# A decoder trunk on one core: values behind logits, queries' transposes behind the probabilities', two fill places a block

## The chip, the cores and the metric

The kernel runs on one core of a Trainium2 chip. The time is device microseconds of one execution of the whole program. The kernel before was run three times: median 1867.74 us, between 1866.12 and 1868.64.

## The reference

Two layers over 1024 tokens of width 1024, all in float32. The first is a gated DeltaNet layer, the second cross-attention in a sliding window of 128 tokens, with 32 query heads of width 64 in groups of eight on 4 key and value heads. The change lies in the second layer. Cut to it:

```python
def swa_sink_mixer(h, w_in, q_gain, sinks, w_out, k_band, v_band, bias, mask):
    q, z = jnp.split(h @ w_in, 2, axis=-1)                       # projections
    q = rms_norm(q.reshape(B, T, B_Q_HEADS, B_HD), q_gain) * (B_HD ** -0.5)
    logits = jnp.einsum("bnqkgd,bnskd->bnkgqs", q, k_band) + bias
    logits = jnp.where(mask, logits, -jnp.inf)
    m = jnp.maximum(jnp.max(logits, axis=-1, keepdims=True), sink)
    p = jnp.exp(logits - m)
    probs = p / (jnp.sum(p, axis=-1, keepdims=True) + jnp.exp(sink - m))
    o = jnp.einsum("bnkgqs,bnskd->bnqkgd", probs, v_band)
    return (o.reshape(B, T, B_W) * jax.nn.silu(z)) @ w_out
```

The tokens come in 8 blocks of 128; the queries of block n see the keys of the blocks n-1 and n.

## The kernel before, in words

Float32 products are made from two halves of each operand, `hi` and `lo`: hi times hi, hi times lo, lo times hi, three matmuls for one.

The second layer's work is cut into 8 head groups (`Group`, four query heads each) of 8 token blocks, 64 blocks in all. A block goes through four pieces on TensorE, and each piece has its followers on other engines:

- `q_turn(i)`: two transposes of the queries (L1149, tile `tp`). ScalarE writes them out as `qT` (L1152), VectorE the rest as `qTl` (L1153).
- `logits(i)`: six pairs of matmuls (L1174, tile `lg`). A pair uses the two halves of the array's rows at the same time. VectorE applies the window (L1178) and adds the bias and takes the extreme `m` (L1182), ScalarE makes the exponentials and their sums (L1187), VectorE the reciprocal `den` (L1189), GpSimd the probabilities `lsb` (L1191).
- `turn(i)`: four transposes of the probabilities (L1197, tile `tp`), written out by ScalarE (L1201) and VectorE (L1205) as `pT`; GpSimd masks the part of the earlier block (L1202).
- `values(i)`: products of `pT` with the values (L1218, tile `pv`), pairs that use the two halves of the array's columns; a block with n = 0 has half as many. ScalarE writes them out as `ot` (L1220).

Between these pieces stand the projections: of the queries (`b_q`, through `gemm_tc`, L983 to L985, 256 columns a matmul) and of the gate z (`b_z`, through `gemm_ct`, L180, L182, L184, 512 columns a matmul), tile `mm`. TensorE's instructions stay in the order in which the code is written. The order is made by `interleave`: the generator `b_attend` is the front and yields a number in places where it can be filled, and the projections are the back and are taken until their costs have used up that number (0.65 for six matmuls of the queries, about 0.22 for one of z). The four pieces of one pass of the loop belong to different blocks: `turn(i)`, `q_turn(i + 3)`, `logits(i + 2)`, `values(i - 1)`. The order on the other engines is set by a scheduler that puts the front's instructions ahead of the back's.

PSUM holds three tiles `tp`, two pairs of `lg`, one `pv` and two `mm`.

Of the kernel before, what the change touches and what calls it, by code (L numbers as in the profile page):

```python
# [64 lines left out]
class Kernel:  # L65
# [1072 lines left out]
    def b_attend(self, groups):  # L1138
# [5 lines left out]
        def q_turn(i):  # L1144
            X, n = blocks[i]
            qv = X.q[n // 4][:, n % 4, :, :].rearrange("p (r a) d -> p r (a d)", a=2)
            ps = aps.tile([P, 4, P], F32, name="tp", bufs=3)[:, 0:2, :]
            for pr in range(2):
                nc.tensor.transpose(out=ps[:, pr, :], in_=qv[:, pr, :], identity=self.ident)  # L1149
            hi = bp.tile([P, 2, P], F32R, name="qT")  # L1150
            lo = bp.tile([P, 2, P], F32R, name="qTl")
            nc.scalar.copy(out=hi, in_=ps)  # L1152
            nc.vector.tensor_tensor(out=lo, in0=ps, in1=self.f32(hi), op=ALU.subtract)  # L1153
            qT[i] = hi, lo
# [38 lines left out]
        def turn(i):  # L1193
            L = Ls.pop(i)
            ps = aps.tile([P, 4, P], F32, name="tp", bufs=3)
            for e in range(4):
                nc.tensor.transpose(out=ps[:, e, :], in_=L[:, e, 0:P], identity=self.ident)  # L1197
            pTs[i] = {}
            if blocks[i][1]:
                pT = pTs[i][0] = bp.tile([P, 4, P], F32, name="pT0")  # L1200
                nc.scalar.copy(out=pT, in_=ps)  # L1201
                nc.gpsimd.affine_select(out=pT, in_=pT, pattern=[[0, 4], [-1, P]], compare_op=ALU.is_gt, fill=0.0,  # L1202
                                        base=0, channel_multiplier=1)
            pT = pTs[i][1] = bp.tile([P, 4, P], F32, name="pT1")
            nc.vector.tensor_tensor(out=pT, in0=ps,  # L1205
                                    in1=self.cst[:, C_TRI:C_TRI + P].unsqueeze(1).broadcast_to([P, 4, P]), op=ALU.mult)

        def values(i):
            X, n = blocks[i]
            g, c = X.hg // 2, n % 4  # L1210
            if c == 0:
                X.ot.append(bp.tile([P, 2, 512], F32, name="ot", bufs=4))
            po = aps.tile([P, 2, P], F32, name="pv", bufs=1)
            pT = pTs.pop(i)
            for kb in sorted(pT, reverse=True):
                v = self.vv[:, n - 1 + kb, g * 64:g * 64 + 64]
                for e in range(2):
                    nc.tensor.matmul(po[e * 64:e * 64 + 64, :, :], v, pT[kb][:, e::2, :],  # L1218
                                     start=(kb == 1), stop=(kb == min(pT)))
            nc.scalar.activation(out=X.ot[-1][:, :, c * P:c * P + P], in_=po, func=AF.Copy, scale=0.5)  # L1220
            if n == NB - 1:
                self.b_done(X)
# [7 lines left out]
        logits(1)  # L1230
        q_turn(2)
        yield 2.5
        fill = (1.2, 1.2, 0.6, 0.6, 1.2)
        steps = iter(())
        for i, (X, n) in enumerate(blocks):
            turn(i)
            yield fill[0]
            if i + 3 <= last:
                q_turn(i + 3)
            yield fill[1]  # L1240
            if i + 2 <= last:
                logits(i + 2)
            yield fill[2]
            if X.hg < 7:
                nxt = groups[X.hg + 1]
                if n == 0:
                    nxt.keys, steps = self.key_stack(nxt.hg // 2) if X.hg % 2 else (X.keys, iter(()))
                    self.b_bias(nxt)
                next(steps, None)
            yield fill[3]  # L1250
            if i:
                values(i - 1)
            yield fill[4]
        values(last)

    def run(self):
# [142 lines left out]
```

## Time and profile before

| what | value |
|---|---|
| median of three runs | 1867.74 us |
| profiled execution, its own time | 1867.72 us |
| its span, first to last instruction | 1866.0 us |
| granted TensorE clock over the span | 0.996 |
| TensorE matmuls, busy | 1809.7 us (97%) |
| VectorE busy | 1231.2 us (66%) |
| ScalarE busy | 730.7 us (39%) |
| GpSimd busy | 514.0 us (28%) |

The busy time is the union of the instructions' spans, from the first to the last instruction of the program. Matmuls overlap in time, so a duration printed for one is longer than the distance to the next; to see how fast TensorE moves, starts are compared with starts. The second layer's attention lies between about 1154 and 1690 us. Before it come the first layer and the keys and values, behind it the output projection.

### The profile page before, as it was taken

How to read it: one execution, taken by the hardware profiler on the slowest of the kernel's cores; microseconds unless marked ns; L12 is line 12 of the kernel's file. 1: busy time of each engine (PE TensorE's matmuls, PEld its weight loads, DVE VectorE, ACT ScalarE, POOL GpSimd, SP SyncE). 2: the span in 40 equal slices, each digit the busy share in tenths (PEclk: the TensorE clock that was granted, in tenths of full speed). 3: DMA queues.
4: the chain of work that ended last, by engine and by line, in shares of the span. 5: the costliest groups of instructions: out<-in, count | busy, mean ns of one | idle time of the engine just before them, and what ended most of it. 6: DMA issues, size and time to landing. Idle time of an engine off the chain costs nothing.

```text
span 1866.0 us, 31106 instructions
## 1 busy us (share of the span) xinstructions
PE 1809.7 (97%) x11778; PEld 1466.0 (79%) x11778; DVE 1231.2 (66%) x2895; ACT 730.7 (39%) x1813; POOL 514.0 (28%) x629
## 2 busy tenths in 40 slices
PE   6999999999999998999999999999999999999999
PEld 6667778787878776778788899887787787777887
DVE  6777776868586778765545365777776766763432
ACT  6446362634445364523112042444444444441100
POOL 1323232323222233221311231333333323221211
PEclk9999999999999999999999999999999999999999
DMA  4611111112011111122655331111111111225552
GB/s 151 134 49 35 57 46 46 47 35 69 23 58 35 58 34 47 45 91 92 236 170 171 122 92 46 30 46 46 63 41 52 57 34 59 68 69 201 182 169 102
DMA packets 134874, 149.55 MB, mean 80 GB/s; under 512 B 7242, under 2 KB 91716, under 8 KB 134724
## 3 DMA queue, kind: packets, MB, share of 16 engines
q1 hardware_dynamic: 124384, 130.40, 22.5%
q10 hardware_dynamic: 10340, 17.16, 2.9%
q8 instruction: 93, 1.52, 0.3%
q14 instruction: 57, 0.47, 0.1%
HBM read 116.05 MB, written 31.49 MB: 79 GB/s over the span
## 4 chain that ended last, share of the span: by engine, by line
PE 77%; DVE 10%; issue 3%; POOL 3%; ACT 1%; DMA 1%; POOLq 0%; DVEq 0%; ACTq 0%; SPq 0%
PE mm L180 9%; PE mm L182 9%; PE mm L184 9%; PE acc L933 6%; PE acc L932 6%; PE acc L931 6%; PE mm L983 4%; PE mm L984 4%; PE mm L985 4%; PE pv L1218 3%; PE lg L1174 3%; DVE acc L494 2%; PE tp L1197 1%; DVE wlo L157 1%; PE kqp L693 1%
## 5 line engine op out<-in xcount | busy, mean ns | idle before, releaser
L180 PE MATMUL mm<-hh,whi 128*128 128x512 f32 (+1 forms) x1040 | 428.0, 412 | 2.5 <-ACT hh L246 2.4
L182 PE MATMUL mm<-hl,whi 128*128 128x512 f32 (+1 forms) x1040 | 417.9, 402 | 1.5 <-DVE hl L247 1.5
L184 PE MATMUL mm<-hh,wlo 128*128 128x512 f32 (+1 forms) x1040 | 415.4, 399 | 0.0
L157 DVE TENSOR_TENSOR wlo<-wraw,whi 128x512 fp32r<-128x512 f32 x292 | 205.8, 728 | 225.0 <-POOL whi L150 192.4
L150 POOL TENSOR_SCALAR whi<-wraw 128x1024 fp32r<-128x1024 f32 x110 | 121.3, 1103 | 474.7 <-PE acc L933 240.7
L180 PEld LDWEIGHTS mm<-hh,whi 128*128 128x128 f32 x1040 | 197.0, 189 | 39.1 <-issue 4.6
L184 PEld LDWEIGHTS mm<-hh,wlo 128*128 128x128 f32 x1040 | 196.9, 189 | 37.3 <-issue 4.2
L182 PEld LDWEIGHTS mm<-hl,whi 128*128 128x128 f32 x1040 | 197.2, 190 | 35.6 <-issue 4.2
L983 PE MATMUL mm<-whi,hh 128*128 128x256 f32 x608 | 183.6, 302 | 0.0
L984 PE MATMUL mm<-wlo,hh 128*128 128x256 f32 x608 | 171.9, 283 | 0.0
L985 PE MATMUL mm<-whi,hl 128*128 128x256 f32 x608 | 171.8, 283 | 0.0
L494 DVE SCALAR_TENSOR_TENSOR acc<-u,cw,acc 128x512 f32<-128x512 f32 x192 | 152.9, 798 | 22.0 <-POOL acc L491 19.6
L1187 ACT ACTIVATE lsb<-lsb,m 128x129 f32<-128x129 f32 x256 | 100.4, 394 | 165.2 <-DVE m L1182 129.3
L983 PEld LDWEIGHTS mm<-whi,hh 128*128 128x128 f32 x608 | 115.8, 190 | 14.7 <-issue 10.0
L1191 POOL TENSOR_TENSOR lsb<-lsb,den 128x512 f32<-128x512 f32 x64 | 72.9, 1139 | 189.2 <-DVE den L1189 177.6
L153 POOL TENSOR_TENSOR wraw<-wraw,gcolb 128x512 f32<-128x512 f32 x72 | 79.0, 1117 | 140.4 <-DMA wraw<-in_b_w_in 96.7
L984 PEld LDWEIGHTS mm<-wlo,hh 128*128 128x128 f32 x608 | 116.1, 191 | 0.2
L985 PEld LDWEIGHTS mm<-whi,hl 128*128 128x128 f32 x608 | 115.8, 190 | 0.0
L491 POOL TENSOR_SCALAR acc<-u,cw 128x512 f32<-128x512 f32 x64 | 57.0, 891 | 183.4 <-ACT u L487 169.9
L931 PE MATMUL acc<-whi,hh 128*128 128x512 f32 x256 | 99.7, 389 | 0.0
L933 PE MATMUL acc<-whi,hl 128*128 128x512 f32 x256 | 99.6, 389 | 0.0
L932 PE MATMUL acc<-wlo,hh 128*128 128x512 f32 x256 | 99.6, 389 | 0.0
(352 smaller groups left out, 3722.0 us busy)
## 6 DMA issues: line engine op xcount, KB each, us to landing
wraw<-in_a_w_in SPq DMA_DIRECT2D x48, 512.0 KB, 4.0
wraw<-in_a_w_out SPq DMA_DIRECT2D x32, 512.0 KB, 3.6
wraw<-in_b_w_in SPq DMA_DIRECT2D x32, 512.0 KB, 4.0
wraw<-in_b_w_out SPq DMA_DIRECT2D x32, 512.0 KB, 3.9
og<-zs SPq DMA_DIRECT2D x32, 256.0 KB, 2.0
ogT<-zs SPq DMA_DIRECT2D x24, 256.0 KB, 2.1
btab<-lt SPq DMA_DIRECT2D x1, 4096.0 KB, 24.3
dm<-gd SPq DMA_DIRECT2D x8, 512.0 KB, 4.1
```

Of the source, the lines that this page charges most:

```text
L150: nc.gpsimd.tensor_scalar(out=hi, in0=raw, scalar1=1.0, scalar2=1.0, op0=ALU.mult, op1=ALU.mult)
L157: nc.vector.tensor_tensor(out=lo[:, ks], in0=raw[:, ks], in1=self.f32(hi[:, ks]), op=ALU.subtract)
L180: nc.tensor.matmul(ps, hi[:, k, :], hh[:, k, :], start=(k == 0), stop=False)
L182: nc.tensor.matmul(ps, hi[:, k, :], hl[:, k, :], start=False, stop=False)
L184: nc.tensor.matmul(ps, lo[:, k, :], hh[:, k, :], start=False, stop=(k == KT - 1))
L494: nc.vector.scalar_tensor_tensor(out=acc, in0=u[:, t:t + 512], scalar=cw[:, t, blk:blk + 1], in1=acc, op0=ALU.mult, op1=ALU.add)
L931: nc.tensor.matmul(ps[c], oh[:, k, ts], hi[:, kk, :], start=(k4 + k == 0), stop=False)
L932: nc.tensor.matmul(ps[c], oh[:, k, ts], lo[:, kk, :], start=False, stop=False)
L933: nc.tensor.matmul(ps[c], ol[:, k, ts], hi[:, kk, :], start=False, stop=(k4 + k == 6))
L983: nc.tensor.matmul(ps, hh[:, k, ts], hi[:, k % 4, :], start=(k == 0), stop=False)
L984: nc.tensor.matmul(ps, hh[:, k, ts], lo[:, k % 4, :], start=False, stop=False)
L985: nc.tensor.matmul(ps, hl[:, k, ts], hi[:, k % 4, :], start=False, stop=(k == KT - 1))
```

## The change

One pass of the loop in `b_attend` is written in another order. `q_turn(i + 3)` follows `turn(i)` without a yield between, `values(i - 1)` follows `logits(i + 2)` without one, and the yields become 2.4, 1.2 and 1.2 in place of 1.2, 1.2, 0.6, 0.6 and 1.2. The key steps and the bias load of the next head group stand behind the values, between the last two yields. Nothing is computed in another way.

```diff
-        fill = (1.2, 1.2, 0.6, 0.6, 1.2)
         steps = iter(())
         for i, (X, n) in enumerate(blocks):
             turn(i)
-            yield fill[0]
             if i + 3 <= last:
                 q_turn(i + 3)
-            yield fill[1]
+            yield 2.4
+
             if i + 2 <= last:
                 logits(i + 2)
-            yield fill[2]
+            if i:
+                values(i - 1)
+            yield 1.2
             if X.hg < 7:
                 nxt = groups[X.hg + 1]
                 if n == 0:
                     nxt.keys, steps = self.key_stack(nxt.hg // 2) if X.hg % 2 else (X.keys, iter(()))
                     self.b_bias(nxt)
                 next(steps, None)
-            yield fill[3]
-            if i:
-                values(i - 1)
-            yield fill[4]
+            yield 1.2
         values(last)
```

The order on TensorE behind the logits of one block, in the kernel before; `mm` rows are projections of z, `lg` logits, `pv` values:

```order
L1174 MATMUL lg<-kl,qT 128x256 x2
L184 MATMUL mm<-hh_85,wlo 128x512
L180 MATMUL mm<-hh_85,whi 128x512
L182 MATMUL mm<-hl_86,whi 128x512
L184 MATMUL mm<-hh_85,wlo 128x512
L180 MATMUL mm<-hh_85,whi 128x512
L182 MATMUL mm<-hl_86,whi 128x512
L1218 MATMUL pv<-pT_12028,vv 64x256 x2
L1218 MATMUL pv<-pT_12025,vv 64x256 x2
```

The same place on TensorE in the changed kernel:

```order
L1174 MATMUL lg<-kl,qT 128x256 x2
L1218 MATMUL pv<-pT_12028,vv 64x256 x2
L1218 MATMUL pv<-pT_12025,vv 64x256 x2
L184 MATMUL mm<-hh_85,wlo 128x512
L180 MATMUL mm<-hh_85,whi 128x512
L182 MATMUL mm<-hl_86,whi 128x512
```

The six projections that stood between the logits and the values stand behind the values. The transposes that follow on TensorE, before; `lsb` are the probabilities, `qr` the queries:

```order
L1197 MATMUL tp<-cst,lsb 128x128 x4
L182 MATMUL mm<-hl_86,whi 128x512
L184 MATMUL mm<-hh_85,wlo 128x512
L180 MATMUL mm<-hh_85,whi 128x512
L182 MATMUL mm<-hl_86,whi 128x512
L184 MATMUL mm<-hh_85,wlo 128x512
L180 MATMUL mm<-hh_85,whi 128x512
L1149 MATMUL tp<-cst,qr 128x128 x2
L182 MATMUL mm<-hl_86,whi 128x512
```

And in the changed kernel:

```order
L1197 MATMUL tp<-cst,lsb 128x128 x4
L1149 MATMUL tp<-cst,qr 128x128 x2
L182 MATMUL mm<-hl_86,whi 128x512
L184 MATMUL mm<-hh_85,wlo 128x512
L180 MATMUL mm<-hh_85,whi 128x512
```

The six projections between the two groups of transposes stand behind both.

## Rows read from the trace of the kernel before

**Rows 1.** Stretches: length; busy of PE, PEld, DVE, ACT, POOL; granted clock; DMA share; GB/s.

```profile
1163.20:1168.80 5.60, 5.60 (x29) 5.24 (x30) 4.93 (x18) 2.47 (x11) 4.02 (x3) 0.50 0.00 0
1170.00:1690.00 520.00, 520.00 (x3701) 415.25 (x3700) 371.23 (x1196) 241.64 (x776) 171.76 (x229) 1.00 0.18 55
```

**Rows 2.** Waits of 1150 to 1690: who waited for whom, total us, times, longest.

```profile
PEld pv L1218 <- issue: 12.9, 36, 0.4
...
PE lg L1174 <- DVE m L1182: 3.2, 2, 1.7
```

**Rows 3.** Timeline of TensorE, logits and values among query projections: start, length, instruction.

```profile
1302.69 0.28 PE L985 MATMUL mm<-whi,hl 128*128 128x256 f32 x1
1302.90 0.38 PE L1174 MATMUL lg<-kh,qT 64*128 64x256 f32 x2
1303.12 0.28 PE L1174 MATMUL lg<-kh,qTl 64*128 64x256 f32 x2
...
1303.60 0.28 PE L1174 MATMUL lg<-kl,qT 64*128 64x256 f32 x2
1303.81 0.39 PE L983 MATMUL mm<-whi,hh 128*128 128x256 f32 x1
1304.03 0.28 PE L984 MATMUL mm<-wlo,hh 128*128 128x256 f32 x1
1304.15 0.28 PE L985 MATMUL mm<-whi,hl 128*128 128x256 f32 x1
...
1305.21 0.28 PE L985 MATMUL mm<-whi,hl 128*128 128x256 f32 x1
1305.42 1.08 PE L1218 MATMUL pv<-pT,vv 128*64 128x256 f32 x8
1306.44 0.39 PE L983 MATMUL mm<-whi,hh 128*128 128x256 f32 x1
1306.66 0.28 PE L984 MATMUL mm<-wlo,hh 128*128 128x256 f32 x1
```

**Rows 4.** Timeline of TensorE, values of a block with n = 0.

```profile
1313.34 0.65 PE L1218 MATMUL pv<-pT,vv 128*64 128x256 f32 x4
1313.92 0.39 PE L983 MATMUL mm<-whi,hh 128*128 128x256 f32 x1
```

**Rows 5.** Timeline of TensorE, logits among z projections of 512 columns.

```profile
1669.34 0.28 PE L1174 MATMUL lg<-kl,qT 64*128 64x256 f32 x2
1669.55 0.50 PE L180 MATMUL mm<-hh,whi 128*128 128x512 f32 x1
1669.88 0.39 PE L182 MATMUL mm<-hl,whi 128*128 128x512 f32 x1
1670.12 0.39 PE L184 MATMUL mm<-hh,wlo 128*128 128x512 f32 x1
```

**Rows 6.** Timeline of TensorE, start of the stage, transposes directly behind logits.

```profile
1157.51 0.27 PE L1174 MATMUL lg<-kl,qT 64*128 64x128 f32 x2
1157.71 0.44 PE L1149 MATMUL tp<-cst,qr 128*128 128x128 f32 x2
1157.91 0.37 PE L983 MATMUL mm<-whi,hh 128*128 128x256 f32 x1
```

**Rows 7.** Timeline of TensorE, transposes among query projections.

```profile
1307.85 0.28 PE L985 MATMUL mm<-whi,hl 128*128 128x256 f32 x1
1307.97 0.60 PE L1197 MATMUL tp<-cst,lsb 128*128 128x128 f32 x4
1308.33 0.36 PE L983 MATMUL mm<-whi,hh 128*128 128x256 f32 x1
1308.53 0.28 PE L984 MATMUL mm<-wlo,hh 128*128 128x256 f32 x1
...
1309.82 0.38 PE L1149 MATMUL tp<-cst,qr 128*128 128x128 f32 x2
1309.96 0.36 PE L983 MATMUL mm<-whi,hh 128*128 128x256 f32 x1
```

## The prediction

> **What bounds the kernel now.** I read the stretch table first, because the page's share of busy time averages over stages and the change touches one: attention of the second layer, from about 1154 us to 1690 us. From 1170 us on TensorE is busy for 520.00 of 520.00 us at a granted clock of 1.00, while VectorE has 371 us of work, ScalarE 242 and GpSimd 172 [rows 1]. Then the waits, to see whether TensorE stands for anyone: its matmul queue waits 3.2 us in all, twice, for the maxima `m` of VectorE, and both waits lie at the start of the stage, before 1170 us; what its weight loads are charged with is "issue", which is a wait for nothing the profile shows [rows 2]. So the stage lasts as long as TensorE's own sequence, and only what happens between two neighbouring matmuls can shorten it. That is why the third view was the timeline of TensorE alone, read by the distance from one start to the next.
>
> In the projections of the queries a matmul of 256 columns follows the last after 0.12 us (1304.03 to 1304.15). At the logits this breaks [rows 3]. The last projection starts at 1302.69, the first pair of logits at 1302.90: 0.21, or 0.09 more than the beat. The second pair starts 0.22 after the first, 0.10 more. The last pair at 1303.60 is followed by a projection at 1303.81, 0.09 more; and the projection after that comes 0.22 later, 0.10 more. The shape printed in the rows says what is special: projections use the array as 128*128, logits as 64*128, value products as 128*64. Each time the shape changes, the next group starts 0.09 us late and its first interval is stretched as well. The values show it too: 0.09 before (1305.21 to 1305.42), 0.10 after the first projection behind them (1306.44 to 1306.66). A block with four value rows lasts 0.58 up to the next projection [rows 4], one with eight 1.02, so four rows (two pairs) are worth 0.44 and 0.58 - 0.44 = 0.14 is overhead: 0.09 of it the late start of what follows, 0.05 the stretched first interval, half as long as the others.
>
> So alone among projections a logits group carries 0.09 + 0.10 + 0.09 + 0.10 = 0.38 us of overhead, and a values group 0.09 + 0.14 + 0.10 = 0.33, together 0.71 us a block. In the stretch with 512-column projections (beat 0.24, 1669.88 to 1670.12) the way out of the logits is the same: the usual 0.12 becomes 0.21, and the first projection takes 0.33 in place of 0.24 [rows 5]. About half of the blocks lie in each stretch.
>
> **The change part by part.** (a) *Values directly behind logits.* The order of instructions on TensorE has this neighbourhood in the blocks 1 to 61 (block 0 has no values before it, the last two no logits): 61 times a return to the 128*128 shape between the two groups disappears. What goes is the 0.09 and 0.10 on the way out of the logits and the 0.09 + 0.05 on the way into the values, 0.33 us. What comes is one direct boundary from 64*128 to 128*64, which before never had. Its bounds: nothing at all if neither shape has to wait for the other, and 0.33 us if it costs as much as both old boundaries. The nearest row is at the start of the stage, where logits are followed directly by transposes: 1157.51 to 1157.71 is 0.20, again 0.09 late, and the two transposes take 0.20 to the next projection [rows 6] where 0.14 is usual [rows 7], so 0.06 more: 0.15 in all. Every boundary in rows 3 is a late start of 0.09, whatever the two shapes, plus a first interval that depends on the incoming group (0.10 for logits and projections, 0.05 for values). I therefore take 0.09 + 0.05 = 0.14 and a gain of 0.33 - 0.14 = 0.19 us a block: 61 x 0.19 = 11.6 us. The ends are 61 x 0.33 = 20.1 us and zero.
>
> On such boundaries the Trainium skill, "TensorEngine Tiling (Array Packing)", section Tiling Modes (Key Properties), says that changing the tiling mode drains TensorE, while changing only the tile does not. The trace agrees as to the late start of 0.09 us at every change of shape. The page names the drain alone; by it the change would save one drain a block, 61 x 0.09 = 5.5 us, and the stretched first interval behind each boundary, which rows 3 show, would not be counted.
>
> (b) *Queries' transposes directly behind the probabilities'.* This looks like the same gain and is not. Transposes have the projections' shape 128*128. Four of them start on the beat (1307.85 to 1307.97), reach the next projection after 0.36 and stretch its first interval to 0.20, 0.08 more [rows 7]: 0.44 for four. Two take 0.14 and the same 0.08: 0.22. That is 0.11 us for each transpose and nothing for the group, so six in a row cost 0.66 = 0.44 + 0.22. I put this part at zero, 61 times.
>
> (c) *Two fill places.* The fill of a block stays 1.2 + 1.2 + 0.6 + 0.6 + 1.2 = 2.4 + 1.2 + 1.2 = 4.8, so the same projections are spread over the same blocks; no matmul is added or removed, and none changes its operands.
>
> (d) *What moves on the other engines.* The pair of `q_turn` evictions (ScalarE `qT`, VectorE `qTl`) comes right behind those of `turn`, and ScalarE's copy of the values `ot` now comes ahead of the four exponentials of the same block, or in front of most of them, instead of between or behind them. The bias loads on SP and the key steps come one place later. All of it is covered by TensorE's projections: the maxima of a block are needed one block later, when its logits' PSUM tiles are reused, its probabilities between one and two blocks later, and the fill between logits and the `turn` that reads them is 7.2 before and after. If that cover went, every late microsecond would be a microsecond of the stage, since TensorE has no slack of its own. I cost it at zero.
>
> The sum: the profiled execution took 1867.72 us, 1866.0 of them the span, and the median of the runs is 1867.74, so the two can be used alike. 1867.7 - 11.6 = 1856.1 us.
>
> **The rivals.**
> *The direct boundary is free.* Rows and columns of the array are split differently in the two groups, and if the values' weights can be brought in under the last logits, all 0.33 us go: 1867.7 - 20.1 = 1847.6 us. Against it: in the rows no change of shape starts on the beat.
> *The direct boundary is dear.* It changes both the row and the column split, which no row shows, and could cost two late starts and two stretched intervals. Between one that leaves 0.09 us of gain (5.5 us, 1862.2) and one that leaves nothing (1867.7). For it speaks only that it was never seen; against it, that 0.09 appears alike at all boundaries of rows 3 and 6.
> *A new wait, and a slow clock behind it (slower).* The one place where TensorE waited is the second block of logits: it needed the PSUM tiles that VectorE had not yet read out, and stood for 3.2 us [rows 2]; behind that the granted clock was 0.50, the 1.2 GHz level, for 5.6 us [rows 1], half of which, 2.8 us, is lost. Such an event costs 6.0 us. Now the evictions come in two bursts in place of four places a block, so VectorE or ScalarE may read out the logits later than before. If the reordering brought one such event at each of the seven changes of head group, where VectorE also has key and gate work, it would cost 42 - 11.6 = 30 us: 1898 us. At two events the gain is gone, and three, 1867.7 - 11.6 + 18 = 1874.1 us, are the nearest clear loss. Against it: after 1170 us the whole 520 us have no such wait, with VectorE busy 71% of the time.
>
> **How the numbers follow.** The forecast, 61 boundaries less at 0.19 us, gets 0.70, with its own range of 1853 to 1860 (0.13 to 0.24 us a block, the rounding of four differences of 0.01 and a microsecond or two of new waits). The free boundary gets 0.10, the dear one 0.15, of which 0.07 for about 1862 and 0.08 for no gain, and the new wait 0.05. What a measurement of this kernel can tell from no change is about 0.2%, 3.7 us. Faster than 1864.0 are the forecast, the free boundary and the milder dear one: 0.87. Within 0.2% is the dear one without gain: 0.08. Slower is the wait: 0.05. The range runs from 1849 to 1863: it holds the forecast, the milder dear boundary and the part of the free one that falls short of its end, and leaves out some 0.18.
>
> **What would show it.** In the profile after, the last pair of logits and the first value product should start about 0.21 us apart, the first interval within the values stay at its present length, and the next projection follow as now. The six transposes should last about 0.58 us to the next projection, 0.36 + 2 x 0.11. The stage should end some 11 to 12 us earlier with TensorE still busy all the time at clock 1.00, and everything after it, the output projection, shift without changing its length. I am wrong if the distance from logits to values is well over 0.21 us or at the beat of 0.12, if waits of TensorE for `m`, `lsb`, `qT` or a free PSUM tile appear after 1170 us, or if the clock falls inside the stage.

## The result and the profile after

The changed kernel takes 1856.36 us (median of five runs, 1851.54 to 1859.02), the kernel before 1867.84 in the runs beside it: 11.5 us less, ratio 0.9935 with a 95% interval of 0.992 to 0.9949. The forecast was 1856.1. Runs with the same mean granted clock, 0.995, lie further apart than the medians: 1856.07 to 1857.62 us with the change, 1868.97 to 1872.03 before (those measured beside e1 to e4).

The stretch of attention and the waits of TensorE in the kernel after, read as [rows 1] and [rows 2]:

```profile
1170.00:1679.00 509.00, 509.00 (x3713) 419.80 (x3713) 369.61 (x1206) 240.97 (x783) 174.92 (x231) 1.00 0.18 56
```

```profile
PE lg L1174 <- DVE m L1182: 3.2, 2, 1.7
...
PEld pv L1218 <- issue: 1.1, 3, 0.4
```

TensorE is busy all the time, as before, at a granted clock of 1.00 once a slow stretch at the start has ended (at about 1172.2 us here), and its matmuls wait for nothing but the maxima at the start, the same 3.2 us. The weight loads of the values were charged with 12.9 us of "issue" before, and with 1.1 us now: 61 of 64 times they no longer follow projections.

The timeline of TensorE in the kernel after, one pass of the loop among query projections; it answers to [rows 3] and [rows 7]:

```profile
1302.41 0.28 PE L985 MATMUL mm<-whi,hl 128*128 128x256 f32 x1
1302.62 0.38 PE L1174 MATMUL lg<-kh,qT 64*128 64x256 f32 x2
1302.85 0.28 PE L1174 MATMUL lg<-kh,qTl 64*128 64x256 f32 x2
...
1303.32 0.28 PE L1174 MATMUL lg<-kl,qT 64*128 64x256 f32 x2
1303.53 1.08 PE L1218 MATMUL pv<-pT,vv 128*64 128x256 f32 x8
1304.55 0.39 PE L983 MATMUL mm<-whi,hh 128*128 128x256 f32 x1
1304.77 0.28 PE L984 MATMUL mm<-wlo,hh 128*128 128x256 f32 x1
1304.89 0.28 PE L985 MATMUL mm<-whi,hl 128*128 128x256 f32 x1
...
1307.38 0.28 PE L985 MATMUL mm<-whi,hl 128*128 128x256 f32 x1
1307.50 0.60 PE L1197 MATMUL tp<-cst,lsb 128*128 128x128 f32 x4
1307.93 0.38 PE L1149 MATMUL tp<-cst,qr 128*128 128x128 f32 x2
1308.07 0.37 PE L983 MATMUL mm<-whi,hh 128*128 128x256 f32 x1
1308.27 0.28 PE L984 MATMUL mm<-wlo,hh 128*128 128x256 f32 x1
```

The direct boundary that no row of before showed: 1303.32 to 1303.53, 0.21, late by the usual 0.09. From there the values last 1.02 to the next projection, as in [rows 3], so their stretched first interval has kept its 0.05. The way from logits back to projections (0.09 and 0.10) is gone. The six transposes take 0.57 to the next projection, whose first interval is then stretched to 0.20, 0.08 more than usual: 0.65 in all, where four and two apart took 0.44 + 0.22 = 0.66.

From the first transposes of the probabilities to the first matmul of the output projection the profile before has 517.92 us (1169.87 to 1687.79) and the one after 504.86 (1172.86 to 1677.72), 13.06 less. What follows is 178.17 and 178.16 us long. The two profiled executions, 1867.72 and 1857.62, differ by only 10.1 us because the attention began 2.84 us later in the second; the code before it is the same, and in the ten profiles of this study its first logits lie anywhere from 1155.9 to 1160.9 us. A part of that is the clock ahead of the attention: the three profiles with the earliest starts (before, e3, e8) have two short stretches at a granted clock of 0.50 there, the changed kernel three, and e5, the latest, five. I therefore compare this stage, called *the stage* below, beside the medians.

### The profile page after: what moved, and what is told of

Read it like the earlier page. It is cut to its first block, busy times and chain, and to the rows that moved or that the text cites. A ratio compares the mean times of both kernels' runs of the same rounds, so it can differ in the third digit from the quotient of the medians.

```text
span 1855.9 us, 31123 instructions
## 1 busy us (share of the span) xinstructions
PE 1798.2 (97%) x11778; PEld 1469.2 (79%) x11778; DVE 1228.8 (66%) x2895; ACT 729.0 (39%) x1813; POOL 518.7 (28%) x629
## 4 chain that ended last, share of the span: by engine, by line
PE 76%; DVE 10%; issue 4%; POOL 3%; ACT 1%; DMA 1%; POOLq 0%; ACTq 0%; DVEq 0%; SPq 0%
PE mm L180 9%; PE mm L182 9%; PE mm L184 9%; PE acc L932 6%; PE acc L933 6%; PE acc L931 6%; PE mm L983 4%; PE mm L985 4%; PE mm L984 4%; PE pv L1218 3%; PE lg L1174 3%; DVE acc L494 2%; PE tp L1197 2%; DVE wlo L157 1%; PE kqp L693 1%
## 5 line engine op out<-in xcount | busy, mean ns | idle before, releaser
L983 PE MATMUL mm<-whi,hh 128*128 128x256 f32 x608 | 178.4, 293 | 0.0
L983 PEld LDWEIGHTS mm<-whi,hh 128*128 128x128 f32 x608 | 116.1, 191 | 11.2 <-issue 10.8
L153 POOL TENSOR_TENSOR wraw<-wraw,gcolb 128x512 f32<-128x512 f32 x72 | 82.7, 1169 | 143.1 <-DMA wraw<-in_b_w_in 77.9
```

The costliest lines, as they stand in the source:

```text
L983: nc.tensor.matmul(ps, hh[:, k, ts], hi[:, k % 4, :], start=(k == 0), stop=False)
```

## The experiments

| kernel | median us | ratio to before (95%) | stage us |
|---|---|---|---|
| before | 1867.84 | | 517.92 |
| the change | 1856.36 | 0.9935 (0.992 to 0.9949) | 504.86 |
| e1 values behind logits alone | 1856.13 | 0.9934 (0.992 to 0.9947) | 505.38 |
| e2 transposes joined alone | 1868.68 | 0.9995 (0.9986 to 1.0004) | 517.50 |
| e3 values behind transposes | 1867.24 | 0.9991 (0.9983 to 1.0) | 517.75 |
| e4 values ahead of logits | 1855.82 | 0.9926 (0.9912 to 0.994) | 504.80 |
| e8 values in two parts | 1874.33 | 1.0031 (1.0021 to 1.0041) | 524.07 |
| e6 values of two blocks | 1849.92 | 0.9907 (0.9894 to 0.9921) | 500.50 |
| e5 later second logits | 1852.48 | 0.9917 (0.9905 to 0.993) | 503.51 |
| e7 e5 and e6 | 1849.48 | 0.99 (0.9886 to 0.9913) | 500.71 |

The runs of before beside e1 to e4 had a median of 1869.46, those beside e5 to e8 1868.57, so ratios are compared. The stage of e5 and e7 can't be set beside the others as it stands: 1.2 of fill was moved ahead of its beginning.

**e1 and e2: which half of the change gains.** All diffs from here on are against the changed kernel, some of them cut; e1 separates the transposes again, e2 the logits and the values.

```diff
             turn(i)
+            yield 1.2
             if i + 3 <= last:
                 q_turn(i + 3)
-            yield 2.4
+            yield 1.2
```

> Only half of the change: values directly behind logits, the queries' transposes in their old place with 1.2 of fill before them; three places a block. Theory (a return to the 128*128 shape between logits and values costs 0.19 us net, joined transposes cost nothing less): the whole gain, 61 x 0.19 = 11.6 us, ratio to before 0.994, as long as the full change. Rival 'breaks' (each interruption of the projections costs the same, the change took two of four away, 11.5 us / 122 = 0.094 us each): only 5.7 us, ratio 0.997.

```diff
                 logits(i + 2)
-            if i:
-                values(i - 1)
-            yield 1.2
+            yield 0.6
...
                 next(steps, None)
+            yield 0.6
+            if i:
+                values(i - 1)
             yield 1.2
```

> The other half alone: queries' transposes directly behind the probabilities', logits and values apart as before with 1.2 of fill between them. Theory: nothing, since transposes have the projections' shape: 61 x 0.01 us at most, ratio 1.000. Rival 'breaks': 5.7 us, ratio 0.997. A rival by the order on the other engines (the joined evictions help or hurt) would show waits of TensorE.

e1 has the whole gain at three places a block, e2 none at three places. Had every interruption of the projections cost the same, the two would have gained alike. TensorE's matmuls wait for nothing after 1170 us in either, so the order on the other engines is no cause.

**e3: two places a block, but no change of shape less.**

```diff
                 q_turn(i + 3)
+            if i:
+                values(i - 1)
             yield 2.4

             if i + 2 <= last:
                 logits(i + 2)
-            if i:
-                values(i - 1)
             yield 1.2
```

> Two places a block as in the change, but the values stand behind the transposes and not behind the logits, so the shape goes 128*128, 128*64, 128*128, 64*128, 128*128: as many changes of shape as before. Theory: no gain, 0.71 us of overhead a block as before, ratio 1.000 (1867 us). Rival 'breaks': the whole gain, 11.5 us, ratio 0.994.

The timeline of TensorE in e3, the way out of the logits and the values behind the transposes:

```profile
1296.25 0.28 PE L1174 MATMUL lg<-kl,qT 64*128 64x256 f32 x2
1296.46 0.38 PE L983 MATMUL mm<-whi,hh 128*128 128x256 f32 x1
1296.68 0.28 PE L984 MATMUL mm<-wlo,hh 128*128 128x256 f32 x1
...
1299.12 0.38 PE L1149 MATMUL tp<-cst,qr 128*128 128x128 f32 x2
1299.44 1.08 PE L1218 MATMUL pv<-pT,vv 128*64 128x256 f32 x8
1300.45 0.39 PE L983 MATMUL mm<-whi,hh 128*128 128x256 f32 x1
1300.67 0.29 PE L984 MATMUL mm<-wlo,hh 128*128 128x256 f32 x1
```

The logits pay their way back to the projections again, 0.21 and 0.22, and the values pay theirs in and out: two transposes and the values' late start take 0.32, where a transpose takes 0.11, so 0.10 too late. As many places as the change, as many changes of shape as before, and the time of before. That is the sharpest of the runs: what counts is how often the array changes its shape, not how often the projections are interrupted.

**e4: the boundary the other way.**

```diff
-            if i + 2 <= last:
-                logits(i + 2)
             if i:
                 values(i - 1)
+            if i + 2 <= last:
+                logits(i + 2)
             yield 1.2
```

> As the change, with values directly ahead of the logits: the direct boundary is crossed the other way, from 128*64 to 64*128. Theory (each change of shape costs a late start of 0.09 us and a first interval that depends on the incoming group alone): 0.14 into the values, 0.19 into the logits, 0.19 into the projections, 0.52 a block as in the change, so 1856 us, ratio 0.994, and the gap from values to logits 0.09 above what it takes without a change of shape. Rival (the direct boundary is cheap only in the direction of the change): up to 0.33 a block, ratio up to 1.000.

The timeline of TensorE in e4, values and logits of one pass:

```profile
1300.60 0.28 PE L985 MATMUL mm<-whi,hl 128*128 128x256 f32 x1
1300.81 1.08 PE L1218 MATMUL pv<-pT,vv 128*64 128x256 f32 x8
1301.82 0.39 PE L1174 MATMUL lg<-kh,qT 64*128 64x256 f32 x2
1302.04 0.28 PE L1174 MATMUL lg<-kh,qTl 64*128 64x256 f32 x2
...
1302.51 0.28 PE L1174 MATMUL lg<-kl,qT 64*128 64x256 f32 x2
1302.72 0.39 PE L983 MATMUL mm<-whi,hh 128*128 128x256 f32 x1
1302.94 0.27 PE L984 MATMUL mm<-wlo,hh 128*128 128x256 f32 x1
```

The values take 1.01 up to the logits, as they took 1.02 up to a projection, and the logits' first interval is 0.22, as in [rows 3]. The price does not depend on the direction, and the stage is as long as with the change (504.80 and 504.86).

**e8: the suspected cost put in once more.** `values` gets a part: the block's own keys stay behind the logits, the earlier keys' part comes after the fill. The diff is cut to the loop.

```diff
             if i:
-                values(i - 1)
+                values(i - 1, 1)
             yield 1.2
+            if i:
+                values(i - 1, 0)
```

> The changed kernel with the suspected cost put in once more: the values' products of a block's own keys stay behind the logits, those of the earlier keys come 1.2 of fill later, so the shape goes to 128*128 and back once more in 55 blocks (block 63 and those with n = 0 excepted). Theory: 55 x (0.09 + 0.10 + 0.09 + 0.05) = 18.2 us over the changed kernel, 1874.5 us, ratio to before 1.004. Rival 'breaks' at 0.094 us: 5.2 us, 1861.6, ratio 0.997.

The timeline of TensorE in e8, the two parts of one block's values (line 1220 there):

```profile
1304.18 0.28 PE L1174 MATMUL lg<-kl,qT 64*128 64x256 f32 x2
1304.39 0.65 PE L1220 MATMUL pv<-pT,vv 128*64 128x256 f32 x4
1304.97 0.39 PE L983 MATMUL mm<-whi,hh 128*128 128x256 f32 x1
1305.20 0.28 PE L984 MATMUL mm<-wlo,hh 128*128 128x256 f32 x1
...
1306.37 0.28 PE L985 MATMUL mm<-whi,hl 128*128 128x256 f32 x1
1306.58 0.65 PE L1220 MATMUL pv<-pT,vv 128*64 128x256 f32 x4
1307.16 0.38 PE L983 MATMUL mm<-whi,hh 128*128 128x256 f32 x1
1307.39 0.28 PE L984 MATMUL mm<-wlo,hh 128*128 128x256 f32 x1
```

1874.33 us against 1874.5 expected; the stage is 19.2 us longer than in the changed kernel, where 18.2 were worked out; where the other 1.0 us comes from stays open. The two parts take 0.58 each, 1.16 together, where one group takes 1.02 [rows 3, 4], and the second part is entered late and left with a stretched projection once more.

**e6: values of two blocks together, a version that beats both.**

```diff
-            po = aps.tile([P, 2, P], F32, name="pv", bufs=1)
-            pT = pTs.pop(i)
-            for kb in sorted(pT, reverse=True):
+            po = aps.tile([P, 2, 2, P], F32, name="pv", bufs=1)
+            for j in range(2):
+                pT = pTs.pop(i + j)
+                for kb in sorted(pT, reverse=True):
...
-            if i:
-                values(i - 1)
+            if i and i % 2 == 0:
+                values(i - 2)
```

> A version that could beat both: values of two blocks together behind every second block's logits, one PSUM tile and one eviction for both, three buffers for the transposed probabilities. Theory: for each pair of blocks one logits group alone (0.38) and one joined group (0.52), 0.90 in place of 1.04, so 30 x 0.14 = 4.2 us less than the changed kernel, 1852 us, ratio to before 0.992. Rival: VectorE, ScalarE or the single values tile make TensorE wait and the gain is lost.

The timeline of TensorE in e6: logits of an odd pass of the loop, then of an even one (values at line 1219 there):

```profile
1291.03 0.28 PE L1174 MATMUL lg<-kl,qT 64*128 64x256 f32 x2
1291.24 0.38 PE L983 MATMUL mm<-whi,hh 128*128 128x256 f32 x1
1291.47 0.28 PE L984 MATMUL mm<-wlo,hh 128*128 128x256 f32 x1
...
1297.76 0.28 PE L1174 MATMUL lg<-kl,qT 64*128 64x256 f32 x2
1297.97 1.95 PE L1219 MATMUL pv<-pT,vv 128*64 128x256 f32 x16
1299.85 0.39 PE L983 MATMUL mm<-whi,hh 128*128 128x256 f32 x1
1300.08 0.28 PE L984 MATMUL mm<-wlo,hh 128*128 128x256 f32 x1
```

Two blocks' values take 1.88, not 2 x 1.02, and every second logits group goes back to the projections by itself. The stage is 4.4 us shorter than with the change, 4.2 expected, and no wait of TensorE's matmuls appears after 1170 us. The ratios to before, 0.9907 against 0.9935, say nearly the same (5.2 us), though each was measured beside its own runs of before and their intervals just touch. The profile of e6 also has a shorter slow stretch at the start, ahead of the stage: behind the same wait of 3.2 us the granted clock is 0.72 over the 6 us from 1163 to 1169, where the changed kernel has 0.50 over such a stretch.

**e5 and e7: the price of a wait at the start.**

```diff
         logits(0)
         q_turn(1)
-        yield 1.5
+        yield 5.2
         logits(1)
         q_turn(2)
-        yield 2.5
```

> The changed kernel with the fill at the start of the stage moved: 5.2 between the first and the second block's logits and none behind them, in place of 1.5 and 2.5 (1.2 more in all, taken from the end). Tests the price of the rival 'a new wait and a slow clock': if TensorE no longer waits 3.2 us for the maxima and no half-clock stretch of some 5.6 us follows, 3.2 + 2.8 = 6.0 us less than the changed kernel, 1850.4 us, ratio to before 0.991. If the clock fell for another reason, only 3.2 us: 1853.2.

> Both of the last two: values of two blocks together and the later second logits. The two act at different places of TensorE's sequence, so the gains should add: 4.2 + 6.0 = 10.2 us less than the changed kernel, 1846.2 us, ratio to before 0.988.

e7 has both edits. Both expectations missed: e5's median lies between the two figures given for it, but not for either reason, and e7 came out 3.3 us above its figure. TensorE's wait in e5, and then the stretch behind the wait in the changed kernel, in e5 and in e7 (columns as in rows 1):

```profile
PE tp L1197 <- POOL lsb L1191: 2.7, 1, 2.7
```

```profile
1166.00:1172.00 6.00, 6.00 (x31) 5.64 (x32) 5.61 (x16) 2.24 (x10) 3.08 (x3) 0.50 0.01 3
```

```profile
1171.00:1174.00 3.00, 1.90 (x16) 1.90 (x17) 2.24 (x7) 1.35 (x4) 1.23 (x2) 1.00 0.00 0
```

```profile
1168.00:1171.00 3.00, 2.27 (x12) 2.27 (x13) 2.24 (x11) 1.72 (x6) 0.87 (x2) 0.68 0.00 0
1171.00:1174.00 3.00, 3.00 (x22) 2.86 (x20) 1.72 (x8) 1.20 (x7) 1.04 (x1) 0.75 0.00 0
```

The second logits no longer wait, but the first transposes of the probabilities, which now follow them without fill, wait 2.7 us for GpSimd's `lsb`. So the wait moved and shrank by 0.5 us. In e5 the clock stayed at 1.00 behind it and the half-clock stretch was saved. From the first logits to the end of the stage e5 takes 514.74 us and the changed kernel 518.30: 3.6 us. In the changed kernel the clock was 0.50 from the end of the wait, at 1165.95, to about 1172.2 us; half of that is 3.1 us, and with the 0.5 of the wait it makes up the 3.6.

In e7 the same wait of 2.7 us was followed by a fall of the clock, but a shorter one, which cost 0.32 x 3 + 0.25 x 3 = 1.7 us. That is as much as e6 lost behind its own wait (0.28 x 6), so e7 had no slow stretch to save and gained next to nothing over e6: from the first logits to the end of the stage 511.99 us against 512.92. So half of a slow stretch is lost, as the prediction has it, but how long the stretch lasts, and whether it comes at all, differs between these single profiles. The idea that the wait could be taken away by moving fill was wrong: what is left is a wait for the first probabilities, which come from the first logits through VectorE, ScalarE and GpSimd. In e5 the transposes that read them start 11.2 us behind those logits (1160.87 to 1172.10), and the fill in between does not last that long.

## Why the prediction was right, by its steps

*What bounds the stage.* Right: TensorE was busy throughout, and only the distances between its starts changed.

*(a), 61 boundaries at 0.19 us, 11.6 us.* Right, and the unknown term was the one chosen by the nearest rows: the direct boundary from 64*128 to 128*64 starts 0.09 late and stretches the first interval by 0.05, 0.14 in all. The stage gained 13.06, more than the 11.6. With three digits for the mean distances in the two traces (0.105 and 0.087 out of the logits, 0.091 into the values, 0.087 at the direct boundary) a block gains 0.196 to 0.199, 12.1 us in all. That the median came within 0.3 us of the forecast is in part luck: the start of the attention alone moves by more than that from one execution to the next.

The prediction left open why the first interval is stretched. The weight loads of the kernel before show it at the place of [rows 3]:

```profile
1302.45 0.19 PEld L984 LDWEIGHTS mm<-wlo,hh 128*128 128x128 f32 x1
1302.58 0.19 PEld L985 LDWEIGHTS mm<-whi,hl 128*128 128x128 f32 x1
1302.90 0.18 PEld L1174 LDWEIGHTS lg<-kh,qT 64*128 64x128 f32 x2
1303.01 0.19 PEld L1174 LDWEIGHTS lg<-kh,qTl 64*128 64x128 f32 x2
```

Among projections a load (PEld) starts together with the matmul ahead of its own: at 1302.58 for the projection at 1302.69. The first load of the logits starts only with its own matmul, at 1302.90, and the second 0.11 behind it. Over the stage the second load follows the first by 0.107 to 0.108 us on the mean at logits and projections, whose stationary tiles have 128 columns, and by 0.055 at the values with 64, in the profiles of before, of the change and of e4 alike. So behind a change of shape the first load is not hidden under an earlier matmul, and the 0.10 and 0.05 are about the distance of the second load from it. This is read from the traces; no run tries it.

*(b), nothing for the joined transposes.* Right by e2: within 0.1% of before, and 0.4 us in the stage.

*The rest of the 13.06* is about 1.0 us. Some 0.7 of it lies in the z projections, whose mean distance fell from 0.2320 to 0.2308 us over the 614 such distances of the changed kernel; no run was made for that, and it stays open.

*(d), covered work on the other engines.* Right: no wait of TensorE for `lsb`, `qT`, `m` or a free tile came up after 1170 us.

*The rivals.* The free and the dear boundary are refuted by the 0.21 us between logits and values and the 1.02 behind it, as long as before. A new wait did not come. Its price of 6.0 us a time was not confirmed as a fixed price: for the clock's part e5 gives about 3.1 us where 2.8 were put, but e6 and e7 have a slow stretch that cost 1.7, behind waits of 3.2 and 2.7 us. The wait's part was not tested by itself, since e5 only moved the wait and left 2.7 of its 3.2 us.

On the drain at a change of tiling mode (the Trainium skill, "TensorEngine Tiling (Array Packing)", section Tiling Modes) the runs agree in so far as a start 0.09 us late is paid at each change, in either direction, and not at transposes, which keep the shape. By the drain alone the change would have gained 5.5 us; the stage's 13.06 shows that the stretched interval behind it counts as well.

## What to carry to other kernels

Where TensorE is the bound, count how often its array changes shape in a pass and put groups with unlike shapes next to each other, so that they share the way out of and back into the common shape; each return saved was worth 0.20 us here, and e6 shows that grouping more work in one shape saves again. Do not count interruptions as such: a group in the projections' own shape, like the transposes, costs only its own matmuls. A boundary that the trace does not show can be put together from a late start and the first interval of the incoming group.

## What the runs showed of the hardware

- At a granted clock of 1.00 a change of shape of the array costs 0.09 us before the next group, whichever the two shapes (128*128, 64*128, 128*64) and whichever the direction, and a first interval longer by 0.10 us for projections and logits and by 0.05 for the value products, whose stationary tile has half as many columns. The spacing of the weight loads behind the change, 0.108 and 0.055 us, fits it; no run varied the columns alone.
- The same wait of 2.7 us of TensorE left the granted clock at 1.00 in e5 and was followed by 0.68 and 0.75 in two stretches of 3 us in e7. The same wait of 3.2 us was followed by 0.50 over 6 us with the change, and by 0.72 over 6 us in e6.
- The time up to the attention varies by up to 5 us between executions of the same code, with two to five short stretches at a granted clock of 0.50 in it, while everything behind it took 178.16 to 178.18 us in all ten profiles.
